# Stick-breaking scans of a unit in two steps with the copy between them, and later first loads of the differential attention

## The chip, the core and the metric

The kernel runs on one core of a Trainium2 chip. A core has a matrix engine (TensorE; PE in the profile, with its weight loads as PEld), VectorE (DVE), ScalarE (ACT), GpSimd (POOL) and SyncE (SP), whose queue issues nearly all transfers between HBM and the on-chip memory. Each engine works through its instructions in their written order, and waits on semaphores of other engines. The metric is the device time of one execution in microseconds.

## The reference

Two layers over 2048 tokens of width 1024. The first layer projects the tokens and mixes three kinds of attention: six heads of stick-breaking attention, six heads of differential attention, and four heads over an external memory. The second has a sliding window in place of the first two. What the change touches is in the first layer:

```python
# stick-breaking, one block of 128 queries
z = einsum(q, k) * scale
log_1mb = where(strict, log_sigmoid(-z), 0.0)
rc = flip(cumsum(flip(log_1mb)))
w = where(strict, exp(log_sigmoid(z) + (rc - log_1mb)), 0.0)
out = einsum(w, v)
...
# differential: two softmaxes per head, their difference weights the values
p = softmax(where(causal, s, NEG_BIG))
a = p[:, :, 0] - lam * p[:, :, 1]
out = einsum(a, v)
```

A stick-breaking weight is the sigmoid of its score times the product of one minus the sigmoids of all later keys up to the query. The kernel takes that running product with a scan from the right.

## The kernel before

The program runs in stages: projections of the first layer, stick-breaking attention, differential attention with part of the output projection mixed in as a filler, the join of the two, then the second layer. Only the second and third stages are touched.

**Stick-breaking** goes over 120 units (p, t, qi, c): a pair of heads p, a chunk t of 512 queries, a block qi of 128 queries in it, and a chunk c of 512 keys, from the last key chunk to the first. A unit has two halves, hh = 0 and 1, one for each head of its pair. What a unit does:

- `scores`: four matmuls (and small mask matmuls on the diagonal) into a bank pair `psz`.
- `weights`: ACT takes two sigmoids of the scores, `s` (of the negative) and `wb`; VectorE scans `s` from the right into the running product `row`, one scan for each half; POOL multiplies `wb` by `row` (line 612).
- `turn`: TensorE transposes `wb`, up to four blocks of 128 for each half, into a bank `pstp`; a copy on ACT or VectorE takes each half's bank to `wT`. There are two such banks for all transposes of the stage.
- `values`: TensorE multiplies `wT` by the values, for two units at a time.

The loop over the units (from line 640) is written by hand: at step k stand `scores` of unit k + 3, `turn` of unit k, `weights` of unit k + 3, and after every second unit `values` of two units. In this stage the written order of SP, PE, DVE and ACT is kept by `PinnedCore`; POOL's is chosen by a scheduler. So on VectorE a unit's two scans stand together, and a copy of `turn` stands ahead of the two scans of the unit three later and behind the two scans of the unit two later. Which engine copies is a pattern, counted through over all copies: `self.tblocks([...], "AAV")`, two on ACT (A) and one on VectorE (V), whichever half it falls on. Helpers record nearly all of this under line 57.

**Differential attention** goes over 24 units (p, k, j) in steps s from −2 on: at step s the scores of unit s + 2, the mixing of unit s + 1 and the values of unit s, cut into four beats, with the filler's pieces between them. A filler piece loads a block of finished mixing outputs (`mp`), casts and splits it (ACT's CAST and line 947 on POOL), and multiplies it by output weights (`psmm<-wo,mp`). Here the order of TensorE and ACT is as written; SP, VectorE and POOL are ordered by the scheduler. Three loads matter: `load_dv` brings the values of a head pair (tile `vc`, four loads of 256 KB for four key chunks), which are first read at step s = 0; `load_dq` brings the queries of the next two units (tiles `qa` and `qd`, eight loads each time), called in `begin()` at the first score of every second unit; and the filler's `load` brings `mp`. All stand in the one queue of SP.

Of the kernel before, what the change touches and what calls it, by code (L numbers as in the profile page):

```python
# [17 lines left out]
P = 128  # L18
# [21 lines left out]
SB_AHEAD = 3  # L40
# [26 lines left out]
class Net:  # L67
# [478 lines left out]
    def stick_breaking(self):  # L546

        nc = self.nc  # L550
        self.nc = PinnedCore(nc, self.tc, ("sync", "tensor", "vector", "scalar"))
        chunks = [(p, t) for p in range(3) for t in range(NT - 1, -1, -1)]
        units = [(p, t, qi, c) for p, t in chunks for qi in range(3, -1, -1) for c in range(t, -1, -1)]
        kv, qs, sls, prs, zs, ws, wTs, pvs = {0: self.sb_first[:2]}, {(0, NT - 1): self.sb_first[2]}, {}, {}, {}, {}, {}, {}

        def begin(p, t):
            sls[p, t] = self.load_silu(self.silu[p], t)
            k = chunks.index((p, t)) + 1
            if k < len(chunks):
                qs[chunks[k]] = self.load_qstack(self.sbq[chunks[k][0]], chunks[k][1])  # L560
            if t == NT - 2 and p < 2:
                kv[p + 1] = self.load_sb(p + 1)
            if p == 2 and t == NT - 1:
                self.fill = self.filler()
                steps.extend(next(self.fill))
                for f in steps[:3]:
                    f()
                del steps[:3]
            if p == 2 and t == NT - 2:
                self.dk, self.dq = {}, {}  # L570
                self.load_dq(0, 0, 0)
                for c in range(NT):
                    self.load_dk(0, c)

        def bounds(u):
            p, t, qi, c = u
            n = (4 * t + qi + 1) * P
            return n, c * 512, min(n, c * 512 + 512)

        def scores(u):  # L580
            p, t, qi, c = u
            n, lo, hi = bounds(u)
            m, diag, s0 = hi - lo, hi == n, int(lo == 0)
            if qi == 3 and c == t:
                begin(p, t)
            if c == t:
                prs[p, t, qi] = [self.t("row", F32, [P, 2048]) for _ in range(2)]
                for hh in range(2):
                    nc.gpsimd.memset(prs[p, t, qi][hh][:, n - 1:n], 1.0)
            z = self.psum("z", [P, 2, 512])  # L590
            for hh in range(2):
                for k in range(2):
                    self.nc.tensor.matmul(z[:, hh, :m], qs[p, t][:, hh, k, qi * P:(qi + 1) * P], kv[p][0][hh][:, lo:hi], start=(k == 0),
                                          stop=(k == 1 and not diag))
                if diag:
                    self.nc.tensor.matmul(z[:, hh, m - P:m], self.identb, self.mask[:, 2 * P + 1:3 * P + 1], start=False, stop=True)
            zs[u] = z

        def weights(u):
            p, t, qi, c = u  # L600
            n, lo, hi = bounds(u)
            m, s0, z = hi - lo, int(lo == 0), zs.pop(u)
            rest = self.t("s", F32, [P, 2, 512])
            self.nc.scalar.activation(rest[:, :, :m], z[:, :, :m], AF.Sigmoid, scale=-0.125)
            w = ws[u] = self.t("wb", F32, [P, 2, 512])
            self.nc.scalar.activation(w[:, :, :m], z[:, :, :m], AF.Sigmoid, scale=0.125)
            for hh in range(2):
                prr = prs[p, t, qi][hh]
                self.nc.vector.tensor_tensor_scan(
                    prr[:, lo + s0 - 1:hi - 1][:, ::-1], rest[:, hh, s0:m][:, ::-1], zero.to_broadcast([P, m - s0]),  # L610
                    prr[:, hi - 1:hi], ALU.mult, ALU.add)
                nc.gpsimd.tensor_mul(w[:, hh, :m], w[:, hh, :m], prr[:, lo:hi])  # L612

        def turn(u):
            n, lo, hi = bounds(u)
            w = ws.pop(u)
            wTs[u] = [self.tblocks([w[:, hh, j:j + P] for j in range(0, hi - lo, P)], "AAV") for hh in range(2)]

        def values(u):
            p, t, qi, c = u  # L620
            n, lo, hi = bounds(u)
            if qi == 3 and c == t:
                pvs[p, t] = self.psum("pv")
            pv, wT, nj = pvs[p, t], wTs.pop(u), (hi - lo) // P
            for j in range(nj):
                for hh in range(2):
                    self.nc.tensor.matmul(pv[64 * hh:64 * hh + 64, qi * P:(qi + 1) * P], kv[p][1][:, 4 * c + j, 64 * hh:64 * hh + 64],
                                          wT[hh][:, j * P:(j + 1) * P], start=(hi == n and j == 0), stop=(c == 0 and j == nj - 1))
            if qi == 0 and c == 0:
                mt = self.t("c2")  # L630
                self.nc.vector.tensor_mul(mt, pvs.pop((p, t)), sls.pop((p, t)))
                self.dma(self.m1[p, :, t * TC:(t + 1) * TC], mt, nc.scalar if p == 2 and t == 0 else None)

        done, steps = 0, []
        zero = self.psum("zero")[:, :1]
        nc.vector.memset(zero, 0.0)
        for u in units[:SB_AHEAD]:
            scores(u)
            weights(u)
        for k, u in enumerate(units):  # L640
            if k + SB_AHEAD < len(units):
                scores(units[k + SB_AHEAD])
            turn(u)
            if k + SB_AHEAD < len(units):
                weights(units[k + SB_AHEAD])
            if steps and (u[0] == 2 and u[1] == NT - 1 and u[3] % 2 and len(steps) > 3 or u[0] == 2 and u[1] == FT):
                steps.pop(0)()
            while k - done >= SB_GROUP or k == len(units) - 1 and done <= k:
                for v in units[done:done + SB_GROUP]:
                    values(v)  # L650
                done += SB_GROUP
        self.nc = nc

    def differential(self):
# [21 lines left out]
                f()  # L676
            del steps[:k]

        for c in (3, 0, 1, 2):
            self.load_dv(0, c)  # L680
        for s in range(-2, len(units)):
            scores, new = self.diff_scores(units[s + 2], rows) if s + 2 < len(units) else ([[]] * 4, [])
            mix = self.diff_mix(units[s + 1], rows) if 0 <= s + 1 < len(units) else [[]] * 4
            turns = self.diff_values(units[s], rows, tail) if 0 <= s else []
            for b in range(4):
                work = [f for c, (both, _) in enumerate(turns) if max(0, c - 1) == b for f in both]
                if turns:
                    pend += [f for c in PRODUCTS[b] for f in turns[c][1]]
                if pend:
                    work.append(lambda fs=pend: take(fs, len(fs)))  # L690
                pend = turns[4][1] if turns and b == 3 else []
                work[2:2] = exps[:2]
                del exps[:2]
                beats += HEAD if s < 0 else 1
                n = max(0, int(total * beats / (4 * (len(units) + 2 * HEAD) * FILL)) - total + len(fill))
                work = mixed(work, fill[:n])
                del fill[:n]
                steps = mixed(scores[b], mix[b])
                if len(scores[b]) == 5 and mix[b]:
                    steps = scores[b][:2] + mix[b][:1] + scores[b][2:3] + mix[b][1:2] + scores[b][3:4] + mix[b][2:] + scores[b][4:]  # L700
                late = b == 0 and 0 < s + 2 < len(units) and units[s + 2][1:] == (0, 0)
                for f in (work + steps if late else mixed(steps, work)):
                    f()
                exps += new[2 * b:2 * b + 2]
                for groups in tail:
                    if groups:
                        for f in groups.pop(0):
                            f()
# [33 lines left out]
    def diff_scores(self, unit, rows):  # L742

        p, k, j = unit
# [3 lines left out]
        def begin():  # L748
            if j == 0:
                self.dsum[p, k] = self.tiny(16, tag="s0", bufs=2)  # L750
            rows[unit] = [], self.tiny(4)
            if j % 2 == 0:
                nxt = [(p_, k_, h) for p_ in range(3) for k_ in range(2) for h in range(2)]
                x = nxt.index((p, k, j // 2)) + 1
# [3 lines left out]
        def chunk(hc, w, c):  # L758
# [3 lines left out]
            if c == 0 and w == 0:  # L762
                if hc == 0:
                    begin()
                rows[unit][0].append((self.t("row"), self.tiny(8, tag="mn", bufs=8)))
            e, mn = rows[unit][0][hc]
            mn = mn[:, 4 * w:4 * w + 4]
# [757 lines left out]
```

## Time and profile before

| what | value |
|---|---|
| median of 3 runs (lowest to highest) | 2526.95 us (2522.09 to 2529.95) |
| the profiled execution: its time, its span | 2526.36 us, 2524.5 us |
| granted TensorE clock, mean over the span | 0.988 |
| stick-breaking, first scan to last value product | 711 to 1050 us |
| differential attention | about 1050 to 1600 us |

Times in the profile are microseconds from the span's start. A row of a group names line, engine, operation, the tiles written and read, and the shapes; behind the bar stand the busy time, the mean duration of one in nanoseconds, and the time that the engine stood idle just before such instructions, with what ended that idle time. In a row of the timeline stand the start, the duration, and in brackets the idle time before it and its end. A wait for several semaphores is put down to the one that came last as far as the profile can tell.

The span is cut into 40 slices of 63 us below; a digit is the busy share of a slice in tenths. Stick-breaking is slices 12 to 17, the differential attention 17 to 26.

```
PE   9999999999999999889888998899999999999998
DVE  4532223542278988799899998684313676777455
ACT  4432222232167877668677777443212777776100
POOL 0401003750068778511111111564511655534332
```

### The profile page before, as it was taken

The page shows a single profiled execution, that of the slowest core. Times are in us where ns is not written, and L with a number is a line of the kernel's source. Part 1 is how long each engine was busy: PE and PEld are TensorE (multiplying, and loading weights), DVE is VectorE, ACT ScalarE, POOL GpSimd, SP SyncE. Part 2 cuts the span into 40 slices and gives each one's busy share as a digit, 9 for nine tenths or more (in the row PEclk, how much of TensorE's full clock was granted, in tenths as well). Part 3 has the DMA queues.
Part 4 walks back from the last instruction along what each step waited for, and adds up shares of the span by engine and source line. Part 5 has one row for each costly group of instructions (what it writes and reads, how often), then busy time and mean ns, then how long its engine had stood idle before and what let it go on. Part 6 is the DMA issues. An engine that isn't in the chain of part 4 may idle for free. (4 is left out here: it accounts for less than half of the span.)

```text
span 2524.5 us, 42315 instructions
## 1 busy us (share of the span) xinstructions
PE 2390.9 (95%) x15564; PEld 1939.1 (77%) x15564; DVE 1572.5 (62%) x3689; ACT 1262.1 (50%) x2459; POOL 939.6 (37%) x768
## 2 busy tenths in 40 slices
PE   9999999999999999889888998899999999999998
PEld 7888998888877777667666676688788777777887
DVE  4532223542278988799899998684313676777455
ACT  4432222232167877668677777443212777776100
POOL 0401003750068778511111111564511655534332
PEclk9999999999999999999999999999999999999999
DMA  8543222342433436734552431553324555532641
GB/s 282 196 142 126 72 87 90 130 138 79 135 87 94 108 85 133 160 90 109 128 134 72 112 87 54 197 183 108 95 89 116 162 151 153 145 102 98 200 149 60
DMA packets 199247, 311.60 MB, mean 123 GB/s; under 512 B 17920, under 2 KB 97280, under 8 KB 198528
## 3 DMA queue, kind: packets, MB, share of 16 engines
q1 hardware_dynamic: 198464, 307.83, 41.2%
q8 instruction: 124, 2.03, 0.4%
q10 hardware_dynamic: 576, 1.05, 0.1%
q14 instruction: 83, 0.68, 0.1%
HBM read 204.74 MB, written 104.07 MB: 122 GB/s over the span
## 5 line engine op out<-in xcount | busy, mean ns | idle before, releaser
L57 PE MATMUL psmm<-big,w 128*128 128x512 f32 x1680 | 413.2, 393 | 0.0
L57 PEld LDWEIGHTS psmm<-big,w 128*128 128x128 f32 x1680 | 305.3, 188 | 57.5
L57 ACT COPY wT<-pstp 128x512 f32<-128x512 f32 (+3 forms) x400 | 203.5, 526 | 188.9 <-PE pstp L57 182.9
L612 POOL TENSOR_TENSOR wb<-wb,row 128x512 f32<-128x512 f32 (+3 forms) x240 | 263.2, 1120 | 70.5 <-DVE row L57 45.4
L57 DVE TENSOR_TENSOR_SCAN row<-s,row,pszero 128x512 f32<-128x512 f32 (+5 forms) x240 | 254.1, 1104 | 38.2 <-ACT s L57 34.6
L254 PE MATMUL psmm<-big,w 128*128 128x512 f32 x1200 | 275.2, 389 | 0.0
L254 PEld LDWEIGHTS psmm<-big,w 128*128 128x128 f32 x1200 | 225.0, 188 | 47.0 <-issue 0.2
L57 PE MATMUL psmm<-big,mp 128*128 128x512 f32 x1056 | 246.0, 393 | 3.4 <-POOL big L1017 3.4
L57 ACT ACTIVATE row<-row,mn 128x2048 f32<-128x2048 f32 (+7 forms) x192 | 229.8, 1202 | 11.5 <-DVE mn L783 7.6
L57 PEld LDWEIGHTS psmm<-big,mp 128*128 128x128 f32 x1056 | 199.1, 190 | 45.4 <-POOL big L1017 3.8
L777 DVE TENSOR_SCALAR_CACHE_REDUCE row<-psz 128x512 f32<-128x512 f32 (+1 forms) x324 | 200.6, 639 | 16.0 <-PE psz L57 15.3
L947 POOL TENSOR_TENSOR mp<-mp,mp 128x640 fp32r<-128x640 f32 x32 | 54.2, 1693 | 347.4 <-ACT mp L57 274.9
L1236 DVE TENSOR_TENSOR c<-psmm,c 128x512 f32<-128x512 f32 x62 | 42.7, 691 | 219.2 <-ACT c L1235 219.1
L57 PE MATMUL psmm<-wo,mp 128*128 128x512 f32 x480 | 148.3, 421 | 6.3 <-ACT mp L57 5.5
L819 DVE SCALAR_TENSOR_TENSOR row<-row,tiny,row 128x128 f32<-128x128 f32 (+7 forms) x144 | 152.6, 1110 | 0.4
L209 POOL TENSOR_TENSOR w<-w,w 128x1024 fp32r<-128x1024 f32 x20 | 48.6, 2429 | 251.3 <-ACT w L208 147.0
L57 PE MATMUL pstp<-ident,wb 128*128 128x128 f32 x816 | 117.3, 276 | 22.8 <-DVE wT L57 15.3
L57 PE MATMUL pstp<-ident,row 128*128 128x128 f32 x816 | 130.4, 281 | 7.8 <-ACT wT L57 6.8
L1235 ACT ACTIVATE c<-psmm 128x512 f32<-128x512 f32 x62 | 36.8, 596 | 189.2 <-PE psmm L254 173.1
L57 PEld LDWEIGHTS pstp<-ident,wb 128*128 128x128 f32 x816 | 91.8, 141 | 43.7 <-POOL wb L612 27.0
L1193 ACT ACTIVATE e<-e,tiny 128x256 f32<-128x256 f32 (+1 forms) x192 | 94.7, 494 | 60.6 <-DVE e L1191 60.1
L57 PEld LDWEIGHTS pstp<-ident,row 128*128 128x128 f32 x816 | 99.4, 143 | 32.5 <-ACT wT L57 14.0
(236 smaller groups left out, 5009.9 us busy)
## 6 DMA issues: line engine op xcount, KB each, us to landing
silu<-c SPq DMA_DIRECT2D x54, 256.0 KB, 2.3
sl<-silu SPq DMA_DIRECT2D x54, 256.0 KB, 3.3
qs<-sbq SPq DMA_DIRECT2D x48, 256.0 KB, 5.3
cs<-rope SPq DMA_DIRECT2D x24, 512.0 KB, 4.2
kc<-k SPq DMA_DIRECT2D x36, 320.0 KB, 5.0
w<-in_we_dram SPq DMA_DIRECT2D x20, 512.0 KB, 3.7
raw<-in_wo_dram SPq DMA_DIRECT2D x20, 512.0 KB, 3.9
rx<-in_x_dram SPq DMA_DIRECT2D x32, 256.0 KB, 2.8
```

The lines of the kernel that those rows point to most:

```text
L57: return self.tc.keep_in_program_order(f(*a, **k))
L209: eng.tensor_sub(lo[:, sl], raw[:, sl], hi[:, sl].bitcast(F32))
L254: self.nc.tensor.matmul(ps, w[a][:, c, :], self.xpart(t, c, b), start=(c == k == 0), stop=(c == 7 and k == 2))
L612: nc.gpsimd.tensor_mul(w[:, hh, :m], w[:, hh, :m], prr[:, lo:hi])
L777: nc.vector.tensor_scalar(e[:, col + lo:col + lo + n0], z[:, :n0], -scale, before, ALU.mult, ALU.min, accum_out=acc)
L819: self.nc.vector.scalar_tensor_tensor(x[:, lo:hi], y[:, lo:hi], cf[hh][:, w:w + 1], x[:, lo:hi], ALU.mult, ALU.add)
L947: self.nc.gpsimd.tensor_sub(ml, m, mh.bitcast(F32))
L1193: nc.scalar.activation(e[:, hh, ns:], e[:, hh, ns:], AF.Exp, bias=nmx[:, hh:hh + 1], scale=-1.0, accum_out=s[:, hh:hh + 1])
L1235: nc.scalar.activation(sg, ps, AF.Sigmoid)
L1236: nc.vector.tensor_mul(sg, ps, sg)
```

## The change

In stick-breaking `weights` now runs only the first half's scan and puts the second into a list `second`. `turn` runs it after the copy of its own first half, so that the second scan of unit k + 2 stands behind the first copy of unit k. The pattern of the copies is now one for each half: "VVA" for the first half, always "A" for the second. In the differential attention the first `load_dv` calls move behind step s = −2, and the next queries are loaded at the third score group of a unit (`hc == 2`) in place of the first.

```diff
-            for hh in range(2):
+
+            def scan(hh):
                 prr = prs[p, t, qi][hh]
                 self.nc.vector.tensor_tensor_scan(
...
                 nc.gpsimd.tensor_mul(w[:, hh, :m], w[:, hh, :m], prr[:, lo:hi])
+            scan(0)
+            second.append(lambda: scan(1))
...
-            wTs[u] = [self.tblocks([w[:, hh, j:j + P] for j in range(0, hi - lo, P)], "AAV") for hh in range(2)]
+            wTs[u] = []
+            for hh in range(2):
+                wTs[u].append(self.tblocks([w[:, hh, j:j + P] for j in range(0, hi - lo, P)], "A" if hh else "VVA"))
+                if second and not hh:
+                    second.pop(0)()
...
-        done, steps = 0, []
+        done, steps, second = 0, [], []
...
         for u in units[:SB_AHEAD]:
             scores(u)
             weights(u)
+            if u != units[SB_AHEAD - 1]:
+                second.pop(0)()
...
-        for c in (3, 0, 1, 2):
-            self.load_dv(0, c)
         for s in range(-2, len(units)):
+            if s == -1:
+                for c in (3, 0, 1, 2):
+                    self.load_dv(0, c)
...
             rows[unit] = [], self.tiny(4)
+
+        def queries():
             if j % 2 == 0:
...
                 if hc == 0:
                     begin()
+                if hc == 2:
+                    queries()
```

VectorE in stick-breaking, before, around 728 to 736 us: `SCALAR_TENSOR_TENSOR row<-s,row,pszero` is a scan; two with the same `s` are the two halves of a unit. The three copies are of the first half of unit 4, the second half of unit 5 and the first half of unit 7.

```order
L57 COPY wT_894_6106<-pstp_893_6102 128x384
L57 SCALAR_TENSOR_TENSOR row_868_5993<-s_897_6114,row_868_5993,pszero_847_5912 128x511
L57 SCALAR_TENSOR_TENSOR row_869_5994<-s_897_6114,row_869_5994,pszero_847_5912 128x511
L57 COPY wT_905_6161<-pstp_904_6156 128x512
L57 SCALAR_TENSOR_TENSOR row_899_6138<-s_906_6163,row_899_6138,pszero_847_5912 128x256
L57 SCALAR_TENSOR_TENSOR row_900_6139<-s_906_6163,row_900_6139,pszero_847_5912 128x256
L57 SCALAR_TENSOR_TENSOR row_899_6138<-s_913_6190,row_899_6138,pszero_847_5912 128x512
L57 SCALAR_TENSOR_TENSOR row_900_6139<-s_913_6190,row_900_6139,pszero_847_5912 128x512
L57 COPY wT_917_6222<-pstp_916_6217 128x512
```

The same place on VectorE with the change: the copies are of the first halves of units 4, 6 and 7.

```order
L57 COPY wT_894_6104<-pstp_893_6100 128x384
L57 SCALAR_TENSOR_TENSOR row_869_5992<-s_890_6089,row_869_5992,pszero_847_5912 128x512
L57 SCALAR_TENSOR_TENSOR row_868_5991<-s_897_6114,row_868_5991,pszero_847_5912 128x511
L57 SCALAR_TENSOR_TENSOR row_869_5992<-s_897_6114,row_869_5992,pszero_847_5912 128x511
L57 SCALAR_TENSOR_TENSOR row_899_6136<-s_906_6163,row_899_6136,pszero_847_5912 128x256
L57 COPY wT_910_6179<-pstp_909_6174 128x512
L57 SCALAR_TENSOR_TENSOR row_900_6137<-s_906_6163,row_900_6137,pszero_847_5912 128x256
L57 SCALAR_TENSOR_TENSOR row_899_6136<-s_913_6190,row_899_6136,pszero_847_5912 128x512
L57 COPY wT_917_6220<-pstp_916_6215 128x512
```

Each copy now stands between the two scans of one unit (those with the same `s`), and the copy of the second half of unit 5 has gone to ACT.

SP where the differential attention begins, before: `vc` are the first values, `qd` the next queries, `mp` the filler's block.

```order
L113 DMA ke_2079_11144<-dfk1_245 32x4x512 x4
L113 DMA vc_1863_10357<-v1_248 128x4x128
L113 DMA vc_1864_10359<-v1_248 128x4x128
L113 DMA vc_1865_10361<-v1_248 128x4x128
L113 DMA vc_1866_10363<-v1_248 128x4x128
L113 DMA qd_1869_10367<-dfq0_241 32x4x256 x4
L113 DMA qd_1870_10372<-dfq0_241 32x4x256 x4
L113 DMA mp_1886_10427<-m1_255 128x3x128
L113 DMA mp_1886_10427<-m1_255 128x2x128
L113 DMA rp_10329<-rx_1874_10382 128x512
```

The same place on SP with the change.

```order
L113 DMA ke_2079_11144<-dfk1_245 32x4x512 x4
L113 DMA qd_1888_10436<-dfq0_241 32x4x256 x4
L113 DMA qd_1889_10441<-dfq0_241 32x4x256 x4
L113 DMA mp_1880_10409<-m1_255 128x3x128
L113 DMA mp_1880_10409<-m1_255 128x2x128
L113 DMA vc_1909_10518<-v1_248 128x4x128
L113 DMA vc_1910_10520<-v1_248 128x4x128
L113 DMA vc_1911_10522<-v1_248 128x4x128
L113 DMA vc_1912_10524<-v1_248 128x4x128
L113 DMA rp_10329<-rx_1868_10364 128x512
```

The four loads of values have moved behind the queries and the filler's block; the queries stay ahead of that block.

## Prediction

> **What bounds the kernel now.** The first line of the page: TensorE is busy nearly all the time, so what the change can win is TensorE's idle time in the two stretches that it touches, or the idle time of VectorE where VectorE sets the pace.
>
> ```profile
> PE 2390.9 (95%) x15564; PEld 1939.1 (77%) x15564; DVE 1572.5 (62%) x3689; ACT 1262.1 (50%) x2459; POOL 939.6 (37%) x768
> ```
>
> Second, the table by windows for stick-breaking (first scan at 711, last value products at 1050); its columns are the window, its length, then PE, PEld, DVE, ACT and POOL busy.
>
> ```profile
> 711.00:1050.00 339.00, 314.99 (x3008) 256.16 (x3010) 296.73 (x331) 267.98 (x405) 273.19 (x338) 0.99 0.44 101
> ```
>
> TensorE idles 24.0 of 339 us. VectorE is next, 296.7 busy and 42.3 idle. Third, the groups of that window; behind the bars stand busy time, mean ns, and the idle time just before, with what ended it.
>
> ```profile
> L57 PE MATMUL pstp<-ident,wb 128*128 128x128 f32 x816 | 117.3, 276 | 22.8 <-DVE wT L57 15.3 <-POOL wb L612 4.5 <-ACT wT L57 1.9
> L57 DVE TENSOR_TENSOR_SCAN row<-s,row,pszero 128x512 f32<-128x512 f32 (+5 forms) x240 | 254.1, 1104 | 38.2 <-ACT s L57 34.6 <-POOL row L589 2.5 <-issue 0.4
> L57 DVE COPY wT<-pstp 128x512 f32<-128x512 f32 (+3 forms) x80 | 47.2, 590 | 4.2 <-PE pstp L57 4.0
> L57 ACT COPY wT<-pstp 128x512 f32<-128x512 f32 (+3 forms) x160 | 82.3, 531 | 68.7 <-PE pstp L57 67.6
> ```
>
> So 22.8 of the 24.0 us stand before the transposes, and 15.3 of them end with a VectorE copy that empties a transpose bank. The 4.5 us put to POOL are mostly the same: here the copy ends at 1043.32, and the transpose starts 0.14 us later.
>
> ```profile
> 1042.65 0.67 DVE L57 COPY wT<-pstp 128x512 f32<-128x512 f32 x1
> 1043.46 0.30 PE L57 MATMUL pstp<-ident,wb 128*128 128x128 f32 x1 [1.26 <-POOL wb L612]
> ```
>
> Fourth, one such wait in the order of time, PE and then DVE, ACT and POOL.
>
> ```profile
> 729.39 1.12 PE L57 MATMUL pstp<-ident,wb 128*128 128x128 f32 x8
> 730.27 1.17 PE L57 MATMUL psz<-kv,qs 128*128 128x512 f32 x4
> 731.28 0.60 PE L57 MATMUL pstp<-ident,wb 128*128 128x128 f32 x4
> 732.82 0.63 PE L57 MATMUL pstp<-ident,wb 128*128 128x128 f32 x4 [0.95 <-DVE wT L57]
> 729.66 2.44 DVE L57 TENSOR_TENSOR_SCAN row<-s,row,pszero 128x511 f32<-128x511 f32 x2
> 732.01 0.67 DVE L57 COPY wT<-pstp 128x512 f32<-128x512 f32 x1
> 731.91 0.59 ACT L57 COPY wT<-pstp 128x512 f32<-128x512 f32 x1 [0.30 <-PE pstp L57]
> 731.09 2.50 POOL L612 TENSOR_TENSOR wb<-wb,row 128x512 f32<-128x512 f32 x2 [0.27 <-DVE row L57]
> ```
>
> The eight transposes of a unit end at 730.51. The copy of the second half is VectorE's, which began two scans at 729.66, so it runs from 732.01 to 732.68. TensorE has only 1.17 us of scores and 0.6 us of transposes to do before it needs that bank, and waits 0.95 us.
>
> Fifth, where the differential attention begins: the SP queue, then ACT, PE and DVE.
>
> ```profile
> 1049.99 4.46 SPq L113 DMA_DIRECT2D vc<-v  x4
> 1055.28 7.84 SPq L113 DMA_DIRECT2D qd<-dfq  x8
> 1063.43 0.38 SPq L113 DMA_DIRECT2D mp<-m  x1
> 1068.66 0.72 ACT L57 CAST mp<-mp 128x640 fp32r<-128x640 f32 x1 [11.83 <-DMA mp<-m]
> 1069.44 0.79 PE L57 MATMUL psmm<-wo,mp 128*128 128x512 f32 x1 [5.53 <-ACT mp L57]
> 1071.80 0.17 DVE L808 RECIPROCAL tiny<-tiny 128x2 f32<-128x2 f32 x1 [7.16 <-ACT row L57]
> ```
>
> A filler block's input (mp) is issued behind the values (vc) and the next queries (qd). ACT stands 11.83 us at its cast, with the exponentials queued behind it; VectorE then waits 7.16 us for these, TensorE 5.53 us for the cast.
>
> **The change, step by step.** *The copies.* The numbers stay: 80 copies on VectorE, 160 on ACT. What moves: second halves always go to ACT, first halves to VectorE in two units of three, and a unit's second scan stands behind that copy. In the case above the copy would be ACT's at 730.51; the sigmoid behind it would be 0.59 us later, which ACT's 71 idle us bear. On VectorE a copy can now meet one scan in progress, not two: at worst 1.22 + 0.67 = 1.89 us after the transposes (half of the 2.44 us pair, plus the copy), where TensorE returns after 1.17 + 0.60 = 1.77 us. That leaves 0.12 us per copy in place of up to 2.44 + 0.67 − 1.77 = 1.34, and nothing in the units in which value products stand between. So at most 15.3 + 4.5 = 19.8 us go. What stays: 80 × 0.12 = 9.6 us if every copy met its worst case, nothing if none did. Only every second unit is without value products, which halves it to 4.8, and not every copy meets the worst case; I take 4.
>
> *The second scan.* It now waits behind a copy that waits for TensorE. Behind it on VectorE stands the next unit's first scan; POOL waits for both, and TensorE for POOL's product. In the case above the pair scanned from 729.66 is multiplied by 733.59, and its transposes start at 736.10:
>
> ```profile
> 736.10 1.04 PE L57 MATMUL pstp<-ident,wb 128*128 128x128 f32 x8
> ```
>
> that is 2.5 us of cover, of which the copy takes 0.67. Where POOL or VectorE runs late the cover is thinner, and it shrinks as TensorE's waits go. The cost is between nothing and what a sixth of the 120 units would lose at 0.67 us each, 13 us; I charge 3, because the one pair shown has cover for three copies. In return the second scan fills the time in which ACT copies and takes the sigmoid, out of the 34.6 us that VectorE waits for ACT now.
>
> Sum of this part: 19.8 − 4 − 3 = **13 us** (between −3 and 19.8).
>
> *The first values and the next queries.* The four vc loads go behind the mp load; the eight qd loads stay ahead of it. Taken away ahead of mp are 4 × 256 KB (DMA issues: count, KB each, median us to landing), at the rate of the window in which the queue drained (last column, GB/s):
>
> ```profile
> vc<-v SPq DMA_DIRECT2D x12, 256.0 KB, 4.5
> mp<-m SPq DMA_DIRECT2D x32, 192.0 KB, 2.6
> mp<-m SPq DMA_DIRECT2D x32, 128.0 KB, 2.6
> 1060.00:1064.00 4.00, 3.26 (x13) 1.97 (x11) 3.31 (x15) 0.00 (x0) 0.00 (x0) 1.00 1.15 222
> ```
>
> 1.05 MB at 222 GB/s is 4.7 us; the issue times give 1055.28 − 1049.99 = 5.3. At the usual 2.6 us to landing ACT would not wait for mp beyond 1061 and all 7.16 us would go; that is the upper end, and half of 5.3 the lower. I take 4.7, since ACT is released by a landing in a queue that stays full. The cast moves from 1068.66 to 1064.0, and VectorE's wait shrinks from 7.16 to 2.4 us. VectorE carries the gain.
>
> [...]
>
> What is late next: the following mp load stands behind vc, which now lands by 1068.7; its cast, at 1073.66 before, should come at 1069.0.
>
> ```profile
> 1073.66 0.71 ACT L57 CAST mp<-mp 128x640 fp32r<-128x640 f32 x1
> L57 PEld LDWEIGHTS pspv<-wT,vc x1632: 132/137/231, 1104.8 to 1595.7; 128*64 128x64 f32 x182
> L57 PEld LDWEIGHTS psz<-kc,qd x32: 186/187/333, 1096.0 to 1135.0; 128*128 128x128 f32 x32
> ```
>
> I charge 0.5 us. The later vc and qd loads themselves cost nothing: their first readers stand at 1104.8 and 1096.0, over 30 us away. The other SP moves (mp ahead of qd at later units) have the same cover. Sum: **4.2 us** (between 2 and 7.2).
>
> *The clock.* After a long wait the granted clock (third column from the right) falls:
>
> ```profile
> 1068.00:1075.00 7.00, 5.16 (x12) 3.69 (x13) 3.20 (x11) 6.10 (x10) 2.05 (x2) 0.51 0.53 176
> 945.00:949.00 4.00, 4.00 (x39) 3.60 (x37) 3.21 (x4) 3.70 (x5) 3.62 (x6) 0.57 0.39 118
> 944.63 1.58 PE L57 MATMUL pstp<-ident,wb 128*128 128x128 f32 x8 [1.87 <-ACT wT L57]
> ```
>
> I add nothing for it: in the first row VectorE is busy for 3.20 us, all that is left after 1071.80, so it sets the pace there. [...] The second row differs: a wait of 1.87 us was enough. [...]
>
> **Sum.** The profiled execution took 2526.4 us (span 2524.5), 0.6 under the median. 2526.4 − 13 − 4.2 = 2509.2, rounded to **2509**. Single measurements of this kernel tell about 0.3%, 7.6 us, from no change.
>
> **The rivals.** *A, the products become the wait.* With TensorE's waits gone VectorE is busy 297 of 326 us and POOL 273; the second scan, always a copy later, brings the product late. If a third of the units lose 0.25 us, the first part gives 3 and not 13: 2519. For it: POOL's share and the thin cover at row ends. Against it: 2.5 us of cover in the steady case.
>
> *B, the copy's wait only changes its place.* As many copies remain on VectorE, and the bank of the first half may be as late as that of the second was. Then only 4.2 us go: 2522. Against it: one scan and not two stands ahead.
>
> *C, slower: VectorE becomes the bound.* Each of the 80 copies can stop VectorE until TensorE's transposes are done. VectorE's 42.3 idle us are used up at 42.3 / 80 = 0.53 us of waiting per copy; at 0.8 us its queue takes 297 + 64 = 361 us, 22 more than now: 2526.4 + 22 − 4.2 = 2544. For it: the copy asks early in every unit. Against it: the copies wait 4.0 us in all today, and the wait for ACT (34.6) shrinks.
>
> *D, more at the second place.* mp lands at once, or the clock matters: 2.5 to 3 us more, 2506.
>
> **Chances.** Forecast 2502 to 2515: 0.57; A (2515 to 2522): 0.18; B (2519 to 2527): 0.10; C: 0.06; D, or less left over at the copies: 0.09. The range takes in the forecast, D and most of A: 2500 to 2520. Faster by over 0.3% (under 2519.4): the forecast, D and most of A, 0.83; within: 0.11; slower: 0.06.
>
> **What would show it.** In the changed profile the row of the pstp transposes should have under 10 us of idle before it, with little from DVE; the scans' wait for ACT s should fall below 34.6; the 711 window should end some 13 us sooner; ACT's cast near the start of the differential attention should wait about 7 and not 11.8 us, and VectorE's reciprocal 2 to 3. If the idle time stands before the same transposes but ends with POOL, it is A; if DVE's copies wait tens of us for PE, C.

## The result, and the profile after

| what | before | after |
|---|---|---|
| median of the runs shown with the result | 2528.45 us (4 runs) | 2501.4 us (4 runs, 2500.09 to 2505.6) |
| ratio of the times, 95% interval | | 0.99 [0.9887, 0.9914] |
| the profiled execution: its time, its span | 2526.36, 2524.5 us | 2500.09, 2498.2 us |

The forecast was 2509 us with a range from 2500 to 2520. The kernel is faster, as forecast; its median lies 8 us below the forecast and 1.4 us above the lower end of the range. In the profiled executions 26.3 us went, where 17.2 were forecast. In the changed kernel line 777 (eviction of scores) has become 791, 808 (reciprocal) 822, 819 (mix) 833, 947 (the filler's subtraction on POOL) 961 and 612 (product) 613.

First the page of the changed kernel, the busy times of its engines.

```profile
PE 2385.3 (95%) x15564; PEld 1937.3 (78%) x15564; DVE 1570.0 (63%) x3689; ACT 1261.4 (50%) x2459; POOL 941.4 (38%) x768
```

The busy times are nearly those of before (VectorE 1570.0 against 1572.5, TensorE 2385.3 against 2390.9): most of what went was waiting. Second, stick-breaking, 16 us sooner at its end: the window (columns as in the prediction) and three groups in it.

```profile
711.00:1034.00 323.00, 310.71 (x3008) 255.27 (x3010) 296.14 (x331) 267.54 (x405) 275.04 (x338) 1.00 0.48 106
```

```profile
L57 DVE TENSOR_TENSOR_SCAN row<-s,row,pszero 128x512 f32<-128x512 f32 (+5 forms) x240 | 255.7, 1106 | 20.6 <-ACT s L57 14.1 <-POOL row L589 3.5 <-issue 1.8
L57 PE MATMUL pstp<-ident,wb 128*128 128x128 f32 x816 | 111.3, 274 | 10.0 <-DVE wT L57 5.4 <-ACT wT L57 1.8 <-POOL row L589 1.7
L57 DVE COPY wT<-pstp 128x512 f32<-128x512 f32 (+3 forms) x80 | 47.3, 592 | 4.2 <-PE pstp L57 3.8
```

The same 3008 matmuls fit into 323 us, not 339. TensorE's idle time fell from 24.0 to 12.3 us, that before the transposes from 22.8 to 10.0, and the part of it that a VectorE copy ends from 15.3 to 5.4. The scans wait 14.1 us for ACT's sigmoid, not 34.6. The copies still wait 4.2 us in all, as before. The remaining 4.3 us are TensorE's busy time (314.99 to 310.71), of which at most 1.7 is the clock that fell at 945 us in the execution before (below). Most of the rest is in the transposes' row, whose busy time fell from 117.3 to 111.3. A VectorE copy interrupts them 10 times now and 26 times before, and in the rows of the prediction eight in one run take 1.04 us, two runs of four 0.60 and 0.63; that the interruptions make the difference is argued from these numbers, not shown.

Third, the start of the differential attention: the SP queue, then ACT, PE and VectorE.

```profile
1033.52 9.04 SPq L113 DMA_DIRECT2D qd<-dfq  x8
1043.16 0.91 SPq L113 DMA_DIRECT2D mp<-m  x2
1044.12 2.99 SPq L113 DMA_DIRECT2D vc<-v  x4
```

```profile
1048.08 0.72 ACT L57 CAST mp<-mp 128x640 fp32r<-128x640 f32 x1 [7.21 <-PE psz L57]
1048.86 0.73 PE L57 MATMUL psmm<-wo,mp 128*128 128x512 f32 x2 [0.88 <-ACT mp L57]
1051.22 0.17 DVE L822 RECIPROCAL tiny<-tiny 128x2 f32<-128x2 f32 x1 [3.12 <-ACT row L57]
```

The filler's block (mp) now stands ahead of the values (vc). ACT's cast waits 7.21 us (11.83 before), TensorE behind it 0.88 (5.53), VectorE's reciprocal 3.12 (7.16). The profile names PE as the end of ACT's wait, but it is the load: its second part landed at 1047.98. VectorE's wait shrank by 4.0 us, and that is what went here.

That makes 20 of the 26.3 us. The rest lies behind, where the prediction saw nothing move. The fourth view is VectorE near 1216 us, first of the kernel before, with PE's and VectorE's waits.

```profile
1216.06 3.79 DVE L819 SCALAR_TENSOR_TENSOR row<-row,tiny,row 128x1024 f32<-128x1024 f32 x3
1219.78 0.68 DVE L777 TENSOR_SCALAR_CACHE_REDUCE row<-psz 128x512 f32<-128x512 f32 x1
1220.52 0.49 PE L57 MATMUL psz<-kc,qd 128*128 128x512 f32 x1 [3.13 <-DVE row L777]
1228.67 0.17 DVE L808 RECIPROCAL tiny<-tiny 128x2 f32<-128x2 f32 x1 [6.25 <-ACT row L57]
```

The same place in the changed kernel:

```profile
1193.16 0.69 DVE L791 TENSOR_SCALAR_CACHE_REDUCE row<-psz 128x512 f32<-128x512 f32 x1
1193.77 3.18 DVE L833 SCALAR_TENSOR_TENSOR row<-row,tiny,row 128x1024 f32<-128x1024 f32 x3
1194.34 0.39 PE L57 MATMUL psz<-kc,qd 128*128 128x512 f32 x1
1200.78 0.17 DVE L822 RECIPROCAL tiny<-tiny 128x2 f32<-128x2 f32 x1 [1.87 <-ACT row L57]
```

The scheduler, which orders VectorE in this stage, put one eviction of scores ahead of three mixes instead of behind them. TensorE no longer waits 3.13 us for that bank, its transposes, ACT's copies and exponentials behind it come sooner, and VectorE waits 1.87 us for these, not 6.25. The three mixes themselves take 3.18 us, not 3.79 (why, is found under e9_onact). No line of the diff speaks of this place.

### The profile page after: what moved, and what is told of

It is laid out like the page before. It is cut to its first block, busy times and chain, and to the rows that moved or that the text cites. A ratio compares the mean times of both kernels' runs of the same rounds, so it can differ in the third digit from the quotient of the medians.

```text
span 2498.2 us, 42275 instructions
## 1 busy us (share of the span) xinstructions
PE 2385.3 (95%) x15564; PEld 1937.3 (78%) x15564; DVE 1570.0 (63%) x3689; ACT 1261.4 (50%) x2459; POOL 941.4 (38%) x768
## 5 line engine op out<-in xcount | busy, mean ns | idle before, releaser
L613 POOL TENSOR_TENSOR wb<-wb,row 128x512 f32<-128x512 f32 (+3 forms) x240 | 265.0, 1120 | 53.4 <-DVE row L57 38.2
L57 DVE TENSOR_TENSOR_SCAN row<-s,row,pszero 128x512 f32<-128x512 f32 (+5 forms) x240 | 255.7, 1106 | 20.6 <-ACT s L57 14.1
L791 DVE TENSOR_SCALAR_CACHE_REDUCE row<-psz 128x512 f32<-128x512 f32 (+1 forms) x324 | 200.3, 640 | 17.4 <-PE psz L57 16.6
L57 PEld LDWEIGHTS pstp<-ident,row 128*128 128x128 f32 x816 | 99.0, 143 | 32.1 <-ACT wT L57 14.1
L57 PE MATMUL pstp<-ident,wb 128*128 128x128 f32 x816 | 111.3, 274 | 10.0 <-DVE wT L57 5.4
L1071 POOL TENSOR_TENSOR mp<-m,mp 128x384 fp32r<-128x384 f32 (+1 forms) x32 | 59.3, 1854 | 143.9 <-PE psmm L57 86.2
```

What stands on the lines that cost most here:

```text
L57: return self.tc.keep_in_program_order(f(*a, **k))
L791: nc.vector.tensor_scalar(e[:, col + lo:col + lo + n0], z[:, :n0], -scale, before, ALU.mult, ALU.min, accum_out=acc)
L1071: nc.gpsimd.tensor_sub(ml, m, mh.bitcast(F32))
```

## The experiments

The median and the ratio come from the timed runs, the ratio against the kernel before on the same chip; the last two columns come from the one profiled execution. "Stick-breaking" is from the start of the first scan to the end of the last value product, "behind it" from there to the end of the span. A single execution is some microseconds less sure than a median: the timed runs of the kernel before lie between 2521 and 2536 us over all experiments.

| kernel | median, us | ratio, 95% interval | stick-breaking | behind it |
|---|---|---|---|---|
| before | | | 340.1 | 1473.9 |
| after | 2501.4 | 0.99 [0.9887, 0.9914] | 324.3 | 1463.6 |
| e1_scans | 2502.46 | 0.9905 [0.989, 0.9921] | 323.1 | 1467.3 |
| e2_loads | 2524.39 | 0.9987 [0.9975, 0.9999] | 340.9 | 1470.6 |
| e3_values | 2500.75 | 0.9887 [0.987, 0.9904] | 323.5 | 1464.2 |
| e5_halves | 2524.48 | 0.9994 [0.9984, 1.0004] | 340.9 | 1469.9 |
| e6_split | 2517.09 | 0.9962 [0.9946, 0.9978] | 333.2 | 1470.9 |
| e7_pin | 2524.22 | 0.9989 [0.9978, 1.0] | 337.9 | 1467.2 |
| e8_pinall | 2513.3 | 0.9948 [0.9933, 0.9963] | 323.3 | 1478.1 |
| e9_onact | 2501.61 | 0.9899 [0.988, 0.9918] | 323.6 | 1463.8 |
| e10_va | 2496.57 | 0.9879 [0.9863, 0.9895] | 317.4 | 1466.7 |
| e11_split | 2485.27 | 0.9827 [0.981, 0.9844] | 323.1 | 1447.7 |
| e12_va_split | 2481.7 | 0.981 [0.9792, 0.9828] | 317.2 | 1449.6 |
| e13_vaa | 2506.0 | 0.9907 [0.989, 0.9925] | 321.2 | 1472.4 |

### The change in its parts

**e1_scans** is the change without its loads; **e2_loads** the loads alone.

```diff
 # e1_scans, against the changed kernel
+        for c in (3, 0, 1, 2):
+            self.load_dv(0, c)
         for s in range(-2, len(units)):
-            if s == -1:
-                for c in (3, 0, 1, 2):
-                    self.load_dv(0, c)
...
                     begin()
-                if hc == 2:
                     queries()
```

> Only the stick-breaking part of the change; the first values and the next queries are loaded as before. Both theories: stick-breaking (first scan to last value product) ends 16 us sooner than before, and at the start of the differential attention ACT's cast waits about 11.8 us and VectorE's reciprocal about 7.2 us for it, as before. Theory ORDER (what was gained behind 1080 us comes mostly from VectorE's order of instructions in the differential attention, which follows the stick-breaking edit: near 1216 us one more eviction of scores stands ahead of three mixes): VectorE's 6.25 us wait there shrinks to about 2, and the profiled execution takes 2505 to 2508 us. Rival LOADS (all that was gained behind 1050 us comes from the later loads): the 6.25 us wait stays, 2510 us.

> Only the later loads of first values and next queries; stick-breaking as before. Both theories: stick-breaking ends when it did before (within 0.5 us); ACT's cast at the start of the differential attention waits about 7.2 us and VectorE's reciprocal about 3.1 us, 4.0 us sooner. Theory ORDER: VectorE's wait of about 6 us near 1216 us stays, and the profiled execution takes 2519.5 to 2522.5 us. Rival LOADS: that wait shrinks to about 2, and it takes 2516 us.

Measured: in these executions the two parts add up. Behind stick-breaking the loads take 3.3 us off (1473.9 to 1470.6), the scans 6.6 (to 1467.3), both 10.3 (to 1463.6). By the medians the loads alone are worth 0.13%, with an interval from 0.01 to 0.25. And the column moves for other edits too: e5_halves, which changes no load and wins nothing in stick-breaking, is 4.0 us shorter behind it, e6_split 3.0. The waits lie as ORDER has them, here ACT's cast at the start and VectorE's reciprocal near 1216 us, of e1_scans and then of e2_loads:

```profile
1051.46 0.72 ACT L57 CAST mp<-mp 128x640 fp32r<-128x640 f32 x1 [12.06 <-DMA mp<-m]
1204.37 0.17 DVE L820 RECIPROCAL tiny<-tiny 128x2 f32<-128x2 f32 x1 [2.88 <-ACT row L57]
```

```profile
1066.20 0.72 ACT L57 CAST mp<-mp 128x640 fp32r<-128x640 f32 x1 [7.44 <-DMA mp<-m]
1227.61 0.17 DVE L813 RECIPROCAL tiny<-tiny 128x2 f32<-128x2 f32 x1 [7.01 <-ACT row L57]
```

LOADS falls: with the scans alone the second wait shrinks and the first stays, with the loads alone it is the other way round. In the totals ORDER was off too: 2502.35 us profiled for e1_scans, where it had 2505 to 2508, and 2524.91 for e2_loads, where it had 2519.5 to 2522.5. VectorE's order in the differential attention is the changed kernel's in e1_scans but for one place at its start, and that of before in e2_loads but for the same place.

Something that is in neither part's code differs as well: the granted clock of TensorE. Here are 32 value products near 1282 us and VectorE's next eviction behind a wait, of the changed kernel and then of e1_scans:

```profile
1282.40 3.68 PE L57 MATMUL pspv<-wT,vc 128*64 128x128 f32 x32
1287.38 0.69 DVE L791 TENSOR_SCALAR_CACHE_REDUCE row<-psz 128x512 f32<-128x512 f32 x1 [3.91 <-PE psz L57]
```

```profile
1285.75 1.97 PE L57 MATMUL pspv<-wT,vc 128*64 128x128 f32 x32
1288.47 0.69 DVE L789 TENSOR_SCALAR_CACHE_REDUCE row<-psz 128x512 f32<-128x512 f32 x1 [1.50 <-PE psz L57]
```

The clock was 0.50 from 1282 to 1286 us in the changed kernel and 1.00 at these products in e1_scans, and VectorE waits 2.4 us longer behind them. e5_halves, e9_onact and e13_vaa have the long form too, the other kernels the short one. So the changed kernel's 1463.6 holds a loss that e1_scans and e2_loads do not have there, and that the parts add up is partly chance.

**e3_values** takes back the later queries alone:

```diff
                 if hc == 0:
                     begin()
-                if hc == 2:
                     queries()
```

> The changed kernel, but the next queries are loaded at the first score group of a unit again, as before; only the first values are later. Theory (the start of the differential attention gains from the values alone, and the queries' place costs and gains nothing): ACT's cast waits 7.2 us and VectorE's reciprocal 3.1 us at the start, as in the changed kernel, and it takes 2499 to 2503 us. Rival (the filler's blocks gain from standing ahead of queries in later units): 2503 to 2507 us.

Measured: 2500.75 us, a cast that waits 7.79 us, a reciprocal that waits 3.71. Where the queries are loaded makes no difference that the runs can tell; as far as they can, the gain of the loads is that of the four first values.

### Why the copies' wait went

**e5_halves** has the new pattern of copies with the scans together, **e6_split** the scans in two steps with the old pattern.

```diff
 # e5_halves, against the kernel before
-            wTs[u] = [self.tblocks([...], "AAV") for hh in range(2)]
+            wTs[u] = [self.tblocks([...], "A" if hh else "VVA") for hh in range(2)]
 # e6_split, against e1_scans
-                wTs[u].append(self.tblocks([...], "A" if hh else "VVA"))
+                wTs[u].append(self.tblocks([...], "AAV"))
```

> Copies by half as in the change (first halves VVA, second halves always A), but a unit's two scans together as before; loads as before. Theory SCANS AHEAD (a copy on VectorE is late by the number of scans ahead of it): every VectorE copy still meets two scans, so PE's idle time before the pstp transposes stays at 18 to 25 us, and stick-breaking ends less than 4 us sooner than before. Rival HALF (what counts is that the copy falls on the first half): the idle time falls to about 10 us, and stick-breaking ends 12 to 16 us sooner.

> The scans in two steps as in the change, but the copies counted through AAV as before; loads as before. Theory SCANS AHEAD: a VectorE copy of a first half meets one scan, one of a second half still two, half of each kind; PE's idle time before the pstp transposes falls from 22.8 to 14 to 18 us, and stick-breaking ends 6 to 9 us sooner. Rival HALF: without the pattern by halves nothing is gained, idle 20 to 25 us, end within 3 us of before.

The transposes' row over 711 to 1050 us, of e5_halves and then of e6_split:

```profile
L57 PE MATMUL pstp<-ident,wb 128*128 128x128 f32 x814 | 115.7, 275 | 23.6 <-DVE wT L57 16.4 <-POOL wb L612 4.8 <-POOL row L589 1.2
```

```profile
L57 PE MATMUL pstp<-ident,wb 128*128 128x128 f32 x816 | 115.3, 276 | 16.6 <-DVE wT L57 14.9 <-POOL wb L613 0.5 <-POOL row L589 0.5
```

SCANS AHEAD holds, HALF falls. The pattern alone wins nothing (340.9 us), the split alone 6.9 us, both together (e1_scans) 17 (340.1 to 323.1): the pattern pays only because it puts every VectorE copy where one scan stands ahead. Of the split alone one thing more can be read: the 4.5 us that the profile puts to POOL are gone, those put to VectorE are not.

**e10_va** and **e13_vaa** give fewer copies to VectorE: "VA" and "VAA" for the first halves, in place of "VVA".

> The changed kernel, with the first halves copied by VectorE and ACT in turn (VA in place of VVA): 60 copies on VectorE, 180 on ACT. Theory: of the idle time that VectorE's copies still end before the pstp transposes (5.4 us) a quarter goes, ACT (267.5 busy of 323) bears 20 copies of 0.53 us more; stick-breaking, 324.3 us long in the changed kernel, takes 322.5 to 324. Rival: ACT's copies now delay its sigmoids, VectorE's wait for these grows above the present 14.1 us, and stick-breaking takes 326 to 330 us. The order of VectorE in the differential attention shifts too, which may move the total by 5 us either way.

> The changed kernel, with one first half in three copied by VectorE (VAA): 40 copies on VectorE, 200 on ACT. Theory that VectorE's copies cost by their number (VVA 324.3 us of stick-breaking, VA 317.4): 313 to 317 us. Rival that ACT is the bound by now (about 267.5 + 40 x 0.53 = 289 us busy, and its sigmoids stand behind the copies): 319 to 326 us. The order of VectorE in the differential attention shifts too, which may move the total by 5 us either way.

```profile
L57 PE MATMUL pstp<-ident,wb 128*128 128x128 f32 x816 | 112.1, 274 | 5.6 <-ACT wT L57 2.3 <-POOL row L589 1.8 <-DVE wT L57 1.0
```

That is e10_va: VectorE's copies now end only 1.0 us of TensorE's waits, and stick-breaking takes 317.4 us, 7 less and not the 2 that were expected at most. The total, 2496.6 us, gains less: behind it the execution is longer (1466.7 against 1463.6), and VectorE's order there is another one. In e13_vaa the next bound shows:

```profile
L57 DVE TENSOR_TENSOR_SCAN row<-s,row,pszero 128x512 f32<-128x512 f32 (+5 forms) x240 | 254.3, 1105 | 38.7 <-ACT s L57 29.8 <-POOL row L589 5.1 <-issue 1.8
```

The scans wait 29.8 us for ACT's sigmoids (14.1 with VVA, 20.4 with VA), and stick-breaking takes 321.2 us: the rival, ACT, is right there. Of the three shares tried VA is the best.

### What changed behind stick-breaking

**e7_pin** is the kernel before with VectorE's order held at one place: one eviction of a unit ahead of its first mixes.

```diff
-                nc.vector.tensor_scalar(e[:, ...], z[:, :n0], ...)
+                (Pinned(nc.vector, self.tc) if (unit, hc, w, c) == ((0, 1, 3), 3, 0, 1) else nc.vector).tensor_scalar(...)
...
-                    self.nc.vector.scalar_tensor_tensor(x[:, lo:hi], ...)
+                    (Pinned(self.nc.vector, self.tc) if (unit, hh) == ((0, 1, 3), 0) else self.nc.vector).scalar_tensor_tensor(...)
```

> The kernel before, with one change in the order of VectorE: in unit (0, 1, 3) of the differential attention one eviction of scores (fourth group of scores, second chunk) is held ahead of the first three mixes of that unit. Stick-breaking and all loads as before. Theory ORDER: PE's wait of 3.1 us and VectorE's wait of 6.25 us near 1220 to 1229 us come from evictions that stand behind mixes; with the eviction ahead PE's wait there goes, VectorE's shrinks below 3 us, all that stands behind 1245 us comes 3 to 5.5 us sooner, and the profiled execution takes 2521 to 2523.5 us. Rival PHASE (the order is only a companion, and the wait comes from when POOL's sums and VectorE's mixes meet): VectorE waits over 5 us there still, 2525.5 to 2527 us.

```profile
1215.22 0.39 PE L57 MATMUL psz<-kc,qd 128*128 128x512 f32 x1
1221.66 0.17 DVE L808 RECIPROCAL tiny<-tiny 128x2 f32<-128x2 f32 x1 [4.96 <-ACT row L57]
```

Half of it came as expected: TensorE's wait is gone, and VectorE's instructions, 2.0 us ahead of the kernel before at 1216 us, are 6.0 ahead at 1250, so the place gave 4.0. But VectorE still waits 4.96 us, near the 5 of the rival. The scheduler moved the three held mixes further back than meant, from 1216 to 1229 us and behind that wait, and the time that they filled is empty there. The profiled execution (2517.7 us) was the fastest of its runs; by the medians e7_pin is 0.11% faster, with an interval that reaches 1.0.

Two kernels made for another question bear on the place more clearly. In e5_halves and e6_split, with the old loads, the scheduler put this eviction and others ahead of the mixes too, and VectorE's reciprocal waits 1.70 and 2.65 us. The row of e5_halves:

```profile
1225.63 0.17 DVE L808 RECIPROCAL tiny<-tiny 128x2 f32<-128x2 f32 x1 [1.70 <-ACT row L57]
```

Counted by ACT's exponentials, the five kernels of this kind (changed, e1_scans, e5_halves, e6_split, e7_pin) gain 3.8 to 5.7 us on the kernel before from 1216 to 1245 us; e2_loads, with the old order there, gains nothing. The place is shown to matter; its exact price is not, since other rows differ too.

**e8_pinall** holds the order written in the program for all such evictions and mixes, in the changed kernel.

> The changed kernel, with VectorE's evictions of the fourth group of scores and the mixes of the first head pair held in the order in which the program is written, in all units. Theory ORDER, taken further: where mixes stood ahead of evictions VectorE's waits (1.87 us at 1200.8, 3.91 us at 1287.4) shrink, and it takes 2495 to 2498 us. Rival: held back like this the mixes come late, and the transposes and value products wait for them: 2500 to 2510 us.

Measured: 2513.3 us, the rival's side and worse than it: 14.5 us more behind stick-breaking. Evictions and reciprocals of VectorE from 1034 to 1600 us, in the changed kernel and in e8_pinall:

```profile
L791 DVE TENSOR_SCALAR_CACHE_REDUCE row<-psz 128x512 f32<-128x512 f32 (+1 forms) x324 | 200.3, 640 | 17.4 <-PE psz L57 16.6
L822 DVE RECIPROCAL tiny<-tiny 128x2 f32<-128x2 f32 x48 | 7.7, 161 | 10.5 <-ACT row L57 10.4
```

```profile
L791 DVE TENSOR_SCALAR_CACHE_REDUCE row<-psz 128x512 f32<-128x512 f32 (+1 forms) x243 | 151.4, 638 | 26.7 <-PE psz L57 26.3
L57 DVE TENSOR_SCALAR_CACHE_REDUCE row<-psz 128x512 f32<-128x512 f32 (+1 forms) x81 | 50.5, 640 | 6.4 <-PE psz L57 5.9
L822 DVE RECIPROCAL tiny<-tiny 128x2 f32<-128x2 f32 x48 | 7.6, 159 | 19.3 <-ACT row L57 19.3
```

The held evictions have a row of their own there (line 57). VectorE waits 33.1 us before evictions, not 17.4, and 19.3 for exponentials, not 10.5; elsewhere mixes seem to fill these waits. "Evictions first" is no rule.

**e9_onact** moves the remaining loads away from mp: the first values and the first unit pair's second queries go out later, from ACT's queue.

> The changed kernel, with the first values (four loads) and the queries of the second half of the first unit pair (eight loads) issued from ACT's queue, later still, so that the filler's block (mp) is issued on SP ahead of both. Theory QUEUE (mp's cast is late because mp stands behind other loads on SP): ACT's cast waits 2 to 4 us and not 7.2, VectorE's reciprocal behind it under 1 us and not 3.1, and all behind comes 2 to 3 us sooner than in the changed kernel: 2497 to 2498 us. Rival: twelve issues more on ACT, about 0.4 us each, hold the exponentials that VectorE waits for, and nothing is won: 2500 to 2503 us.

ACT's cast in e9_onact, and then the mixes from 1034 to 1105 us in the changed kernel and in e9_onact:

```profile
1043.88 0.73 ACT L57 CAST mp<-mp 128x640 fp32r<-128x640 f32 x1 [3.58 <-DMA mp<-m]
```

```profile
L833 DVE SCALAR_TENSOR_TENSOR row<-row,tiny,row 128x1024 f32<-128x1024 f32 (+5 forms) x18 | 19.1, 1116 | 0.1
```

```profile
L833 DVE SCALAR_TENSOR_TENSOR row<-row,tiny,row 128x1024 f32<-128x1024 f32 (+5 forms) x18 | 22.9, 1328 | 0.1
```

At its place QUEUE is right: the cast waits 3.58 us, the reciprocal not at all, and VectorE is 3.8 us ahead of the changed kernel at 1052 (0.6 of it from stick-breaking). At 1105 it is 1.0 ahead, and the total is the same, 2501.61 us. Neither theory had the cause: the same 18 mixes take 3.8 us longer. What that is shows in single rows, POOL's subtraction and a mix of 896 columns, before and after:

```profile
1115.67 1.73 POOL L947 TENSOR_TENSOR mp<-mp,mp 128x640 fp32r<-128x640 f32 x1 [11.47 <-ACT mp L57]
1115.90 2.45 DVE L819 SCALAR_TENSOR_TENSOR row<-row,tiny,row 128x896 f32<-128x896 f32 x1
```

```profile
1095.68 1.15 DVE L833 SCALAR_TENSOR_TENSOR row<-row,tiny,row 128x896 f32<-128x896 f32 x1
1095.74 2.50 POOL L961 TENSOR_TENSOR mp<-mp,mp 128x640 fp32r<-128x640 f32 x1 [12.69 <-ACT mp L57]
1096.75 0.69 DVE L791 TENSOR_SCALAR_CACHE_REDUCE row<-psz 128x512 f32<-128x512 f32 x1
```

Before, POOL started first and the mix took 2.45 us, until 0.95 after POOL's end at 1117.40. After, the mix was 0.06 us ahead; it took 1.15, and POOL took 2.50. The eviction behind it, which reads a bank of scores, ran beside POOL in its usual 0.69. From 1076 to 1120 us the kernel before has four such lengthened mixes (1.24 to 1.31 us each), the changed kernel and e1_scans two in the same stretch of the program, e9_onact five from its start on.

**e11_split** cuts POOL's subtraction into five, **e12_va_split** does so in e10_va.

```diff
-                self.nc.gpsimd.tensor_sub(ml, m, mh.bitcast(F32))
+                for c in range(5):
+                    self.nc.gpsimd.tensor_sub(ml[:, c], m[:, c], mh[:, c].bitcast(F32))
```

> The changed kernel, with the filler's subtraction on POOL (mp<-mp,mp, 640 columns, 1.55 us) cut into five of 128 columns. In the changed kernel 13 of VectorE's 144 mixes take 0.35 to 1.37 us longer than the shortest of their size while such a subtraction runs, 14.5 us in all. Theory LOCK (whichever of the two starts first runs to its end, and the other waits): a mix now waits for at most a piece of about 0.35 us; the 14.5 us fall below 6, and it takes 2490 to 2496 us. Rival SHARE (both only run slower while they overlap): the 14.5 us stay at 12 to 16, and it takes 2499 to 2503 us.

> The kernel with the first halves copied by VectorE and ACT in turn (VA), and the filler's subtraction on POOL cut into five. LOCK: 2486 to 2492 us (2496.6 without the cut). SHARE: 2495 to 2498 us.

Mixes in the differential attention and the subtraction, of the changed kernel and then of e11_split:

```profile
L833 DVE SCALAR_TENSOR_TENSOR row<-row,tiny,row 128x128 f32<-128x128 f32 (+7 forms) x144 | 149.5, 1088 | 0.4
L961 POOL TENSOR_TENSOR mp<-mp,mp 128x640 fp32r<-128x640 f32 x32 | 54.8, 1712 | 334.7 <-ACT mp L57 254.1 <-PE psz L57 45.6 <-DMA qa<-dfq 12.6
```

```profile
L833 DVE SCALAR_TENSOR_TENSOR row<-row,tiny,row 128x128 f32<-128x128 f32 (+7 forms) x144 | 139.7, 1020 | 0.4
L962 POOL TENSOR_TENSOR mp<-mp,mp 128x128 fp32r<-128x128 f32 x160 | 87.0, 576 | 303.0 <-ACT mp L57 229.5 <-PE psz L57 41.6 <-PE psmm L57 13.8
```

LOCK holds, and gives more than expected: 2485.3 us, 16 less than the changed kernel, though VectorE's order is the same row for row and POOL now works 32 us more. The mixes take 9.8 us less, so that some 4.7 of the 14.5 are left; the evictions behind them wait 11.2 us for scores, not 17.4. From 1034 to 1105 us 18 mixes take 17.5 us in e11_split, against 19.1. The filler's subtraction is not the only instruction beside which mixes take longer: six mixes of the changed kernel take 0.8 us longer beside another one on POOL (c<-c,tiny), which was not cut. e12_va_split, 2481.7 us and below its forecast too, is the fastest kernel of the study.

## Why the prediction was right, and where its sizes were off

- **The copies.** "19.8 us go, I take 4 left at the copies": 5.4 are left, the wait of the scans for ACT fell from 34.6 to 14.1, the copies wait no longer than before. The reason given, one scan ahead and not two, is shown by e5_halves and e6_split.
- **The second scan**, charged with 3 us. The idle time before the transposes fell by 12.8 us (22.8 to 10.0), which is 19.8 − 4 − 3: the two charges together were right, though they divide otherwise. Besides the 5.4 us at the copies, POOL's product still ends one wait of 0.7 us (seven waits, 4.5 us before), and POOL's memset of a new `row` (line 589) ends 0.9 us more than before.
- **Stick-breaking** gave 16 us and not 13, and the term that the sum did not have is TensorE's busy time, 4.3 us less. Six kernels with the new scans and copies took 323.1 to 324.3 us, three with the old ones 337.9 to 340.9.
- **Rivals.** A (the products become the wait) and B (the wait only moves) fell: the idle time before the transposes is 10.0 us, and POOL's product ends 0.7 of it. C (VectorE the bound) fell: its copies wait 4.2 us in all, where 0.53 us each was the point.
- **The first values.** Forecast 4.2 us between 2 and 7.2; the place gave 4.0, and the loads alone 3.3 to the end, in one execution. The cast waits "about 7" (7.21), the reciprocal "2 to 3" (3.12). mp, issued from 1043.16 on, landed 4.8 us later, at 1047.98, behind a full queue (DMA share 1.15 from 1043 to 1048 us) and not after the usual 2.6, so D, as far as it rested on a landing at once, fell. The clock stayed whole there (1.00 from 1047 to 1054 us, 0.51 behind the wait before), and the place gave no more for it: that half of D, an estimate that no run shows, fell too, and the prediction's reason, that VectorE sets the pace, fits.
- **The queries** cost and gained nothing, as forecast and as far as e3_values can tell.
- **The step that failed** is the sum itself, "2526.4 − 13 − 4.2", with its sentence "The other SP moves ... have the same cover": everything behind 1072 us was carried over unchanged. There VectorE's order is a scheduler's, and the scans' edit alone changed it in six places; with the times at which mixes meet POOL's subtractions this is most of the 6.6 us between 1473.9 and 1467.3. In e1_scans 3.3 us come between 1085 and 1130 us, where two lengthened mixes of 1.3 us fewer stand, and 4.0 near 1216; later stretches take 0.7 back. That these causes make all of the 6.6 is argued from the traces, not shown: the traces put the order at one place at 3.8 to 5.7, e11_split shows the meetings to cost 10 us and more in the whole stage, the clock near 1282 us moved a further 2.4, and none of these splits the 6.6.
- **Luck.** The two places that the prediction worked out gave 20 us, which alone would have made about 2506, inside the 2502 to 2515 that it held most likely. The other 6 us stand in no term of the sum. They took the median just out of that band; the range, whose lower end was meant for D, still held it by 1.4 us and the profiled execution by 0.1.

## What to carry to other kernels

A copy on an in-order engine is late by what stands ahead of it: put it between two long operations rather than behind both, and see that every copy falls there, since here the pattern alone won nothing and the split alone 6.9 of 17 us. Where a scheduler orders an engine, an edit far ahead can reorder it later, for better or worse; compare the order over the whole program, and separate the parts by kernels that have one each before crediting an edit with the total. And when a gain at one place is given back within 50 us, look for the same instructions running longer, not only for waits.

## What the runs showed of the hardware that was not expected

- A mix on VectorE (`row<-row,tiny,row`) and the filler's subtraction on POOL did not run side by side where they met. In the changed kernel's profile the eleven mixes that started behind a subtraction ended 0.62 to 1.09 us after its end, each about 0.2 us less than the shortest mix of its size takes (0.80 to 1.27); the eleven subtractions that started behind a mix ended 1.40 to 1.47 us after its end, where one that meets no mix takes 1.55 to 1.59. One of the eleven mixes: POOL from 1192.85 for 1.56 us, a mix of 1024 columns started at 1193.77 and took 1.72, that is 1.08 after POOL's end. Why they take turns, no run shows. e11_split puts a price on it: cutting one instruction into five took 16 us off 2501. POOL's pieces of 128 columns take 0.576 us each in the mean, 2.9 for five, against 1.71 for the whole.
- The granted clock fell behind waits of about 2 us. The window shows it near 945 us for the kernel before and not, in the same code, for e7_pin (third column from the right):

```profile
940.00:955.00 15.00, 13.13 (x114) 10.82 (x113) 12.01 (x14) 10.51 (x17) 11.61 (x12) 0.89 0.38 102
```

```profile
940.00:955.00 15.00, 13.33 (x128) 10.82 (x127) 13.89 (x15) 12.32 (x18) 13.49 (x15) 1.00 0.38 106
```

  The kernel before lost 0.11 of 15 us, 1.7 us, e7_pin nothing. The wait of TensorE ahead of it was not the same: 1.87 us in the kernel before (the prediction shows it), 2.61 in e2_loads, where the window's clock was 0.89 too, and 1.19 in e7_pin:

```profile
944.36 1.12 PE L57 MATMUL pstp<-ident,wb 128*128 128x128 f32 x8 [1.19 <-ACT wT L57]
```

  Near 1282 us it fell behind 2.19 us in the changed kernel and was whole behind 1.06 in e1_scans. The length alone did not decide it: in the changed kernel a wait of 1.92 us, which ended at 1356.21, had a clock of 1.00 behind it, from 1354 to 1360. So a wait that differed by 0.7 to 1.1 us between two executions came with a fall of the clock in one and not in the other, and a forecast should not count on either.
